# One core, one decoder layer: feed-forward operands made ahead of the change of stage, conformer norm as a task of its own

## The chip, the core and the metric

The kernel runs on one core of one Trainium2 chip. The metric is the device time of one execution in microseconds (us). Five engines work from queues of their own: PE (matmuls; its weight loads are listed as PEld), DVE (elementwise work), ACT (activations, copies with a scale), POOL, which has next to nothing to do here, and SP, whose queue issues every DMA of this kernel. Each engine takes its instructions strictly in the order in which they were emitted, so an instruction that waits also holds up all that stand behind it.

## The reference

One layer on 2048 tokens of width 1024, all in float32:

```python
h = rms_norm(x, mix_norm_g);  z = h @ w_in                    # 1024 -> 2048
lru_x, lru_gate, conf_a, conf_b = split(z, 4)                 # 512 each
y_lru = rg_lru(conv4(lru_x)) * gelu(lru_gate)
c = silu(layer_norm(conv31(conf_a * sigmoid(conf_b))))
x = x + concat(y_lru, c) @ w_out
x = x + cross_attention(rms_norm(x), mem)                     # 256 memory tokens, 4 heads
g, u = split(rms_norm(x) @ w_up, 2)                           # 1024 -> 2 x 3072
x = x + (gelu(conv3(g)) * u) @ w_down                         # 3072 -> 1024
out = rms_norm(x) * final_norm_g
```

## The kernel before

**Arithmetic.** A float32 operand is split into a rounded high part and a low part: `split` is one ACT copy (`wh`, `Xh`, `hidh`, `yh`) and one DVE subtraction (`wl`, `Xl`, `hidl`, `yl`). `mm3` then makes three matmuls, high by high, high by low, low by high. Nearly all matmuls are 128 x 128 by 128 x 512.

**Stages.** Tokens are worked in four quarters of 512. `mixer(q)` makes the input projection, the conformer convolution (31 DVE instructions for each of four channel blocks) and the LRU of a quarter. `attend(q)` first calls `conf_out`, the layer norm of the conformer branch: two sums over channels made on PE by a matrix of ones (`ps<-sum,ones`), then scale, `Silu` and split. It goes on with the output projection (`ps<-wh,yh` and the like), attention through memory tiles prepared once, the residual, and the normed and transposed rows `xn` that the feed-forward reads; these go to DRAM through `xn_kept`, and the residual through `x2_kept`. `memory_a` and `memory_vo` prepare the memory side meanwhile.

**Feed-forward.** It works on two halves `h` of 1024 tokens, each as a 2 x 2 block of Strassen's kind, seven products for eight. `halves_x(h)` reads the half's sixteen `xn` tiles, makes four combinations (`t`) for each of four contraction blocks and splits all seven operands (`B11`, `B21`, `T2`, `T1`, `T3`, `T4`, `B22`), 28 pairs of tiles. `up(h)` runs over 12 column groups `j`; each has a gate half and an up half, each of them one `strassen_cols` of seven products of 12 matmuls. Raw `w_up` columns come by DMA, are combined (`s`) and split. Its results (`cv`) go to DRAM as `hid`. `prepare_down` makes the seven combinations of `w_down` for its 3 chunks x 4 blocks, splits them (84 pairs) and stores them as `w_down2`; it is started when half 1 of the up projection begins. `down(h)` runs over 3 chunks; each has seven products, each of 4 token blocks x 12 matmuls, whose left operands are loads `h` from `hid` or combinations `s` of them, and whose right operands are loads `wh`, `wl` from `w_down2`. It adds into 16 `acc` tiles, all loaded from `x2` ahead of its first product. `finish` norms and stores.

**What sets the order.** The program is recorded by coroutines (`Task`), where `yield n` asks to be resumed after n us of recorded PE work, and a yielded task waits for that one; `drive` always steps the first due task in its list. The recorded operations then go through a planner (`Program`): buffers come from four pools of fixed slots (`SLOTS`: 82 of S, tiles of 512 columns; 4 of W, raw weights; 4 of D, tiles of 1152 columns for `cb`, `gb`, `cv`; 8 PSUM banks), granted in the order of recording, and a list scheduler places each operation on its engine by due times worked backwards from the PE order. The emitted order of each engine is what it finds. The profile gives every planned instruction the line of the one `getattr` call in `emit`, so groups are told apart by tile names.

Of the kernel before, what the change touches and what calls it, by code (L numbers as in the profile page):

```python
# [41 lines left out]
SLOTS = dict(S=82, W=4, D=4, ps=8)  # L42
# [370 lines left out]
def hybrid_layer(  # L413
# [583 lines left out]
    mixed = [None] * NQ  # L997
    attended = [Task(None) for _ in range(NQ)]
# [42 lines left out]

    def attend(q, ready):
        for t in ready:
            yield t
        C, L = mixed[q]
        Y = []
        yield from conf_out(C, Y)
# [75 lines left out]
    def halves_x(h, B):  # L1123
        for i in range(KH):
            b11, b21 = (xn_kept.get((2 * h) * NK + k) for k in (i, i + KH))
            b12, b22 = (xn_kept.get((2 * h + 1) * NK + k) for k in (i, i + KH))
            t1 = combine("t", b12[:], b11[:], ALU.subtract)
            t2 = combine("t", b22[:], t1[:], ALU.subtract)
            t3 = combine("t", b22[:], b12[:], ALU.subtract)
            t4 = combine("t", b21[:], t2[:], ALU.subtract)  # L1130
            for key, src in (("B11", b11), ("B21", b21), ("T2", t2), ("T1", t1), ("T3", t3), ("T4", t4), ("B22", b22)):
                hi, lo = pair("X")
                split(src[:], hi, lo)
                B.setdefault(key, []).append((hi, lo))
            yield 0

    def strassen_cols(c0, B, outs):
# [10 lines left out]
        def product(bank, src, key, start):  # L1148
            wh, wl = pair("w", (P, KQ, P))
            split(src, wh, wl)  # L1150
            with together():
                for k in range(KH):
                    x = B[key][k]
                    mm3(bank[:], wh[:, k, :], wl[:, k, :], x[0][:], x[1][:], start and k == 0, k == KH - 1, skip_group_check=True)

# [37 lines left out]
    def up(h, B):  # L1193
        for j in range(NCH):
# [31 lines left out]
            yield from strassen_cols(DFF + 2 * j * P, B, gated)  # L1226
# [5 lines left out]
    NCK = 3  # L1232
    KD = NF // NCK // 2
# [6 lines left out]
    def prepare_down():  # L1240
        for c in range(NCK):
            for i in range(KD):
                f = c * 2 * KD + i
                r1, r2 = (raw_rows(w_down[0], (f + j * KD) * P) for j in range(2))
                b11, b12, b21, b22 = r1[:, :TT], r1[:, TT:], r2[:, :TT], r2[:, TT:]
# [12 lines left out]
    def down(h):  # L1258

        acc = [[[x2_kept.get(((2 * h + th) * NTB + tb) * 2 + half, None, "acc") for half in range(2)] for tb in range(NTB)] for th in range(2)]  # L1260
        for c in range(NCK):
            raw = {}

            def hid(kq, th, i):
                if (kq, th, i) not in raw:
                    f = (c * 2 + kq) * KD + i
                    t = tmp("h")
                    t0 = (2 * h + th) * TT
                    pr.dma(t[:], h_kept[f * P : (f + 1) * P, t0 : t0 + TT], reads=[h_tok[h, f]])
                    raw[kq, th, i] = t  # L1270
                return raw[kq, th, i]

            s = {}

            def operand(key, i):
                if (key, i) not in s:
                    if key == "S1":
                        s[key, i] = combine("s", hid(0, 1, i)[:], hid(1, 1, i)[:], ALU.add)
                    elif key == "S2":
                        s[key, i] = combine("s", operand("S1", i)[:], hid(0, 0, i)[:], ALU.subtract)  # L1280
                    elif key == "S3":
                        s[key, i] = combine("s", hid(0, 0, i)[:], hid(0, 1, i)[:], ALU.subtract)
                    elif key == "S4":
                        s[key, i] = combine("s", hid(1, 0, i)[:], operand("S2", i)[:], ALU.subtract)
                    else:
                        return hid(*dict(A11=(0, 0), A12=(1, 0), A22=(1, 1))[key], i)
                return s[key, i]

            def product(banks, akey, bkey, start):
                L, R = [], []  # L1290
                for i in range(KD):
                    src = operand(akey, i)
                    hi, lo = pair("hid")
                    split(src[:], hi, lo)
                    L.append((hi, lo))
                    at = wd_at(c, bkey, i)
                    R.append((wd_kept.get(at, None, "wh"), wd_kept.get(at + 1, None, "wl")))
                for tb in range(NTB):
                    ts = slice(tb * P, (tb + 1) * P)
                    with together():  # L1300
                        for i in range(KD):
# [79 lines left out]
    def nothing():  # L1381
        yield 0
# [49 lines left out]
```

## Time and profile before

| | us |
|---|---|
| median of 3 runs (lowest, highest) | 2584.69 (2583.64, 2588.04) |
| the profiled execution: its time | 2585.25 |
| its span, first to last instruction | 2583.5 |
| PE busy in the span | 2481.4 (96%) |
| DVE busy | 1861.4 (72%) |
| ACT busy | 1119.9 (43%) |
| DMA moved | 522.71 MB, mean 202 GB/s |

Busy PE is the union of matmuls that overlap, and a matmul counts as busy also while the clock is halved; so the share is not the last word on how full PE is. The views of stretches give, for each engine, its busy time with the number of instructions that began in it ("x443"), the clock that TensorE was granted (1.00 is full), and how busy the DMA engines were. Comparing the number of matmuls begun in a stretch with that in a stretch that nothing disturbs gives what the stretch lost, to waits and to the clock together. The view of waits has, per pair of engine and releaser, the total in us, how often, and the longest.

### The profile page before, as it was taken

What the parts mean: (1) busy time and instruction counts of PE and PEld (TensorE: products, weight loads), DVE (VectorE), ACT (ScalarE), POOL (GpSimd) and SP (SyncE); (2) the same over time, 40 slices, a digit from 0 to 9 for tenths busy, and PEclk for the clock granted to TensorE, in tenths of its full rate; (3) what the DMA queues carried; (4) which work ended last, traced back from release to release, by engine and by line L of the source; (5) the groups of instructions that cost most, each with busy time, mean ns of one, the idle gap of its engine ahead of it and who ended that gap; (6) DMA issues with size and microseconds to landing.
All of it is one profiled execution on the core that took longest, in us unless ns stands there. A gap on an engine that the chain in (4) does not pass through costs nothing.

```text
span 2583.5 us, 32715 instructions
## 1 busy us (share of the span) xinstructions
PE 2481.4 (96%) x11300; PEld 2045.9 (79%) x11300; DVE 1861.4 (72%) x3137; ACT 1119.9 (43%) x1939; POOL 0.7 (0%) x6
## 2 busy tenths in 40 slices
PE   7999899998999999999999999899999999998998
PEld 6797788887888787878888887677788878886886
DVE  6999995099529933367667667999976765657656
ACT  6571754226333624355444445565544432223212
POOL 0000000000000000000000000000000000000000
PEclk9999999999999999999999999999999999998999
DMA  8687594855574748533222224689832197779774
GB/s 291 211 270 266 171 321 156 318 164 199 194 251 144 260 139 296 197 107 103 89 90 78 78 90 130 231 314 333 290 102 90 66 330 231 254 271 323 233 240 170
DMA packets 312764, 522.71 MB, mean 202 GB/s; under 512 B 29916, under 2 KB 107740, under 8 KB 312598
## 3 DMA queue, kind: packets, MB, share of 16 engines
q1 hardware_dynamic: 312598, 520.62, 59.1%
q8 instruction: 89, 1.46, 0.2%
q14 instruction: 77, 0.63, 0.1%
HBM read 384.19 MB, written 136.31 MB: 201 GB/s over the span
## 4 chain that ended last, share of the span: by engine, by line
PE 71%; DVE 10%; DMA 3%; issue 2%; ACT 1%; DVEq 0%; ACTq 0%; SPq 0%
PE ps L389 71%; DVE conv L389 2%; DVE wl L389 2%; DVE xc L389 1%; DVE cv L389 1%; DVE s L389 1%; DVE t L389 1%; DMA wh<-w_down 0%; DMA wl<-w_down 0%; DVE gb L389 0%; ACT xn L389 0%; DVE Xl L389 0%; DMA w_down<-wl 0%; DVE gate L389 0%; DMA w_down<-wh 0%
## 5 line engine op out<-in xcount | busy, mean ns | idle before, releaser
L389 PE MATMUL ps<-Xh,wl 128*128 128x512 f32 x1344 | 527.4, 392 | 11.1 <-DVE wl L389 11.0
L389 PE MATMUL ps<-Xh,wh 128*128 128x512 f32 x1344 | 526.6, 392 | 8.2 <-ACT wh L389 5.8
L389 PE MATMUL ps<-Xl,wh 128*128 128x512 f32 x1344 | 525.1, 391 | 0.0
L389 DVE SCALAR_TENSOR_TENSOR conv<-cb,v,conv 128x512 f32<-128x512 f32 x480 | 331.1, 739 | 0.4
L389 PEld LDWEIGHTS ps<-Xh,wl 128*128 128x128 f32 x1344 | 253.2, 188 | 72.2 <-DVE wl L389 20.2
L389 PEld LDWEIGHTS ps<-Xh,wh 128*128 128x128 f32 x1344 | 253.3, 189 | 65.1 <-ACT wh L389 11.0
L389 PEld LDWEIGHTS ps<-Xl,wh 128*128 128x128 f32 x1344 | 253.3, 188 | 52.3
L389 PE MATMUL ps<-wh,hidh 128*128 128x512 f32 x672 | 264.3, 393 | 13.8 <-ACT hidh L389 13.8
L389 PE MATMUL ps<-wh,hidl 128*128 128x512 f32 x672 | 264.1, 393 | 0.0
L389 PE MATMUL ps<-wl,hidh 128*128 128x512 f32 x672 | 263.7, 392 | 0.3 <-DMA wl<-w_down 0.2
L389 DVE TENSOR_TENSOR acc<-acc,ps 128x512 f32<-128x512 f32 x192 | 129.2, 685 | 165.8 <-PE ps L389 165.8
L389 DVE TENSOR_TENSOR wl<-raw,wh 128x512 fp32r<-128x512 f32 x276 | 183.1, 682 | 73.5 <-ACT wh L389 51.6
L389 ACT ACTIVATE wh<-raw 128x512 fp32r<-128x512 f32 x276 | 169.1, 630 | 129.2 <-PE ps L389 68.3
L389 PE MATMUL ps<-xh,wh 128*128 128x512 f32 x512 | 202.2, 395 | 3.9 <-DVE ztail L389 3.1
L389 PE MATMUL ps<-xh,wl 128*128 128x512 f32 x512 | 200.7, 392 | 0.0
L389 PE MATMUL ps<-xl,wh 128*128 128x512 f32 x512 | 200.6, 392 | 0.0
L389 ACT ACTIVATE wh<-s 128x512 fp32r<-128x512 f32 x192 | 118.8, 630 | 113.6 <-DVE s L389 68.5
L389 DVE TENSOR_TENSOR wl<-s,wh 128x512 fp32r<-128x512 f32 x192 | 129.8, 686 | 47.0 <-ACT wh L389 45.5
L389 PEld LDWEIGHTS ps<-wh,hidh 128*128 128x128 f32 x672 | 127.5, 190 | 42.0 <-ACT hidh L389 15.7
L389 ACT ACTIVATE junk<-x 128x512 f32<-128x512 f32 x96 | 60.6, 631 | 215.0 <-DVE x L389 204.0
L389 ACT ACTIVATE u<-ps 128x512 f32<-128x512 f32 x144 | 85.9, 596 | 155.7 <-PE ps L389 150.3
L389 PEld LDWEIGHTS ps<-wh,hidl 128*128 128x128 f32 x672 | 127.2, 189 | 28.8 <-DVE hidl L389 2.6
(190 smaller groups left out, 4310.9 us busy)
## 6 DMA issues: line engine op xcount, KB each, us to landing
raw<-in_w_up_dram SPq DMA_DIRECT2D x96, 512.0 KB
wh<-w_down SPq DMA_DIRECT2D x168, 256.0 KB
wl<-w_down SPq DMA_DIRECT2D x168, 256.0 KB
wh<-w_in SPq DMA_DIRECT2D x96, 256.0 KB
wl<-w_in SPq DMA_DIRECT2D x96, 256.0 KB
hid<-cv SPq DMA_DIRECT2D x48, 512.0 KB
h<-hid SPq DMA_DIRECT2D x96, 256.0 KB
w_down<-wh SPq DMA_DIRECT2D x84, 256.0 KB
```

What stands on the lines that cost most here:

```text
L389: getattr(e, name)(*[resolve(a) for a in args], **{k: resolve(a) for k, a in kw.items()})
```

## The change

- `SLOTS`: S from 82 to 85, D from 4 to 3.
- `conf_out` moves from the start of `attend(q)` into a new task `normed(q)`. For quarter 0 it waits for `mixers[0]` and 40 us; for quarter 1 for `mixers[2]` and `attended[0]`; for quarter 2 for `mixers[3]` and `attended[1]`; for quarter 3 for `normed(2)` and 55 us. `attend(0)` no longer waits for `mixers[1]`.
- `halves_x` becomes the class `HalfX`, which makes an operand when asked. For half 0 the first four operands (`first_x`) are made while the last attention runs, the others when first used. For half 1 the task `kept` makes the four combinations during half 0 of the up projection and stores them to DRAM (`tx`); in the last `strassen_cols` of half 0, `used(key)` splits the half 1 operand of a key as soon as half 0 has used that key.
- `prepare_down` starts with half 0 in place of half 1, is paced with `yield 8` in place of `yield 2`, and loads its raw rows into S tiles (`wd`, four of 256 KB) in place of W tiles (two of 512 KB).
- `down` becomes the class `Down`. `ahead` makes the operands of its first two products during the last `strassen_cols` of half 1. An `acc` tile is loaded when first added to. Half 1 takes the chunks in reverse and begins each with the seventh product, so its first product takes over the weights `wh`, `wl` that half 0 used last.

The diff, cut to its core:

```diff
-SLOTS = dict(S=82, W=4, D=4, ps=8)
+SLOTS = dict(S=85, W=4, D=3, ps=8)
...
+    def normed(q, ready, wait):
+        for t in ready:
+            yield t
+        yield wait
         C, L = mixed[q]
         Y = []
         yield from conf_out(C, Y)
+        mixed[q] = Y, L
...
+        def kept(self):
+            keys = ("T2", "T1", "T3", "T4")
+            k = Kept("tx", 4 * KH, F32)
+            yield attends[NQ - 1]
+            for i in range(KH):
+                b = {key: self.one(key, i) for key in ("B11", "B12", "B22")}
+                t1 = combine("t", b["B12"][:], b["B11"][:], ALU.subtract)
...
+                k.put(i, t2[:])
+                k.put(KH + i, t1[:])
+                yield 20
...
         def product(bank, src, key, start):
+            X = B.get(key)
             wh, wl = pair("w", (P, KQ, P))
...
+            if used:
+                used(key)
...
+    PACE = 8
...
     def prepare_down():
+        yield attends[NQ - 1]
...
-                    yield 2
+                    yield PACE
...
-        acc = [[[x2_kept.get(((2 * h + th) * NTB + tb) * 2 + half, None, "acc") for half in range(2)] for tb in range(NTB)] for th in range(2)]
...
+        def ahead(self, c, n, given=None):
+            self.given = {(c, n): given} if given else {}
+            self.ready[c, n] = self.gather(c, n)
...
+        def add(self, banks, th, half):
+            for tb in range(NTB):
+                at = (th, tb, half)
+                if at not in self.acc:
+                    self.acc[at] = x2_kept.get(((2 * self.h + th) * NTB + tb) * 2 + half, None, "acc")
...
     def feed_forward():
-        yield attended[3]
-        B = {}
-        yield from halves_x(0, B)
-        yield from up(0, B)
-        yield attends[3]
-        B = {}
-        yield from halves_x(1, B)
+        yield first
+        yield attended[NQ - 1]
+        spawn(X[1].kept(), tail)
         spawn(prepare_down(), tail)
-        yield from up(1, B)
-        del B
+        yield from up(0, X[0], X[1].make)
+        downs = [Down(h) for h in range(NH)]
+
+        def ahead(key):
+            if key in ("B21", "T1"):
+                downs[0].ahead(0, ("B21", "T1").index(key))
+
+        yield from up(1, X[1], ahead)
         for h in range(NH):
-            acc = yield from down(h)
-            tasks.insert(0, Task(finish(h, acc)))
+            yield from downs[h].run(downs[h + 1] if h < NH - 1 else None)
+            tasks.insert(0, Task(finish(h, downs[h].acc)))
```

How the emitted order moves, at three places. First SP's queue where the up projection of half 1 ends and the down projection begins; `hid<-cv` are stores of the up projection, all else loads. Before:

```order
L389 DMA raw<-in_w_up_dram 128x4x256 x2
L389 DMA hid<-cv 128x1024 x2
L389 DMA acc<-x_88 128x512 x16
L389 DMA h<-hid 128x512 x2
L389 DMA wh<-w_down_91 128x512
L389 DMA wl<-w_down_91 128x512
L389 DMA wh<-w_down_91 128x512
```

And now:

```order
L389 DMA raw<-in_w_up_dram 128x4x256 x2
L389 DMA h<-hid 128x512
L389 DMA hid<-cv 128x1024
L389 DMA wh<-w_down_91 128x512
L389 DMA wl<-w_down_91 128x512
L389 DMA h<-hid 128x512
L389 DMA hid<-cv 128x1024
L389 DMA wh<-w_down_91 128x512
```

The sixteen `acc` loads stood ahead of the first `h`; now 24 loads (8 `h`, 8 `wh`, 8 `wl`) stand ahead of the first `acc`, and the first of them ahead of two stores of the up projection.

Second DVE's queue where half 1 of the up projection takes over; `t` are half 1's combinations, `Xl` its split operands, `gb`, `up` and `cv` are still work of half 0's last column group. Before:

```order
L389 TENSOR_TENSOR up<-u,ps 128x512
L389 TENSOR_TENSOR t<-xn,t 128x512
L389 TENSOR_TENSOR t<-xn 128x512
L389 TENSOR_TENSOR cv<-cv,up 128x512
L389 TENSOR_TENSOR t<-xn,t 128x512
L389 TENSOR_TENSOR Xl<-xn,Xh 128x512 x3
L389 TENSOR_TENSOR Xl<-t,Xh 128x512
L389 TENSOR_TENSOR t<-xn 128x512 x2
```

And now:

```order
L389 TENSOR_TENSOR gb<-u,ps 128x512
L389 TENSOR_TENSOR Xl<-xn,Xh 128x512 x2
L389 TENSOR_TENSOR wl<-t,wh 128x512
L389 TENSOR_TENSOR Xl<-xn,Xh 128x512
L389 TENSOR_TENSOR wl<-raw,wh 128x512
L389 TENSOR_TENSOR Xl<-xn,Xh 128x512
L389 TENSOR_TENSOR gb<-u,ps 128x512
```

The combinations are gone from this place (the `t` of `wl<-t` belongs to `prepare_down`), and the first `Xl` stand among the last adds of the gate half (`gb`), where they stood behind the first `up` of the up half.

Third PE's queue where attention of quarter 2 ends; `xn` is transposed there for the feed-forward, `sum,ones` is the conformer norm of quarter 3 and `wh,yh` its output projection. Before:

```order
L389 MATMUL ps<-wl,pth 128x512
L389 MATMUL ps<-wh,ptl 128x512
L389 MATMUL ps<-ident,xn 128x128 x16
L389 MATMUL ps<-sum,ones 128x512
L389 MATMUL ps<-ident,xn 128x128 x16
L389 MATMUL ps<-wh,yh 128x512
```

And now, around the first transposes, with 33 matmuls of the same output projection ahead of these rows, up to the last of `ptl`:

```order
L389 MATMUL ps<-wh,yh 128x512
L389 MATMUL ps<-wl,yh 128x512
L389 MATMUL ps<-wh,yl 128x512
L389 MATMUL ps<-ident,xn 128x128 x16
L389 MATMUL ps<-wh,yh 128x512
```

The two `sum,ones` of quarter 3 have moved far ahead, into the attention of quarter 2, and 36 matmuls of the output projection now stand between the last matmul with `ptl` and the first transposes.

More of the change, by code (lines that the diff above doesn't have):

```diff
@@ L997, in hybrid_layer @@
     mixed = [None] * NQ
+    started = [Task(None) for _ in range(NQ)]
     attended = [Task(None) for _ in range(NQ)]
@@ L1040, in mixer @@
         mixed[q] = C, L
+    def normed(q, ready, wait):
+        for t in ready:
+            yield t
+        yield wait
+        C, L = mixed[q]
+        Y = []
+        yield from conf_out(C, Y)
+        mixed[q] = Y, L
     def attend(q, ready):
@@ L1044, in attend @@
             yield t
-        C, L = mixed[q]
-        Y = []
-        yield from conf_out(C, Y)
+        Y, L = mixed[q]
+        started[q].done = True
         xs = load_x(q, "x1")
@@ L1121, in combine @@
         return t
[L1123 to L1131, printed above, removed]
+    UP_ORDER = ("B11", "B21", "T2", "T1", "T3", "T4", "B22")
@@ L1243, in prepare_down @@
                 f = c * 2 * KD + i
-                r1, r2 = (raw_rows(w_down[0], (f + j * KD) * P) for j in range(2))
-                b11, b12, b21, b22 = r1[:, :TT], r1[:, TT:], r2[:, :TT], r2[:, TT:]
+                raw = []
+                for r0 in (f * P, (f + KD) * P):
+                    for half in range(2):
+                        t = tmp("wd")
+                        pr.dma(t[:], w_down[0, r0 : r0 + P, half * TT : (half + 1) * TT])
+                        raw.append(t[:])
+                b11, b12, b21, b22 = raw
                 t1 = combine("t", b12, b11, ALU.subtract)
@@ L1255, in prepare_down @@
                     wd_kept.put(at + 1, lo[:])
-                    yield 2
-    def down(h):
-        acc = [[[x2_kept.get(((2 * h + th) * NTB + tb) * 2 + half, None, "acc") for half in range(2)] for tb in range(NTB)] for th in range(2)]
[L1261 to L1301, printed above, removed]
-                            mm3(banks[tb][:], L[i][0][:, ts], L[i][1][:, ts], R[i][0][:], R[i][1][:], start and i == 0, i == KD - 1, skip_group_check=True)
-                    yield 0
-            def add(banks, th, half):
-                for tb in range(NTB):
-                    t = acc[th][tb][half]
-                    V("tensor_tensor", t[:], t[:], banks[tb][:], op=ALU.add)
-            pa = [ps() for _ in range(NTB)]
-            yield from product(pa, "A11", "B11", True)
-            add(pa, 0, 0)
-            pb = [ps() for _ in range(NTB)]
-            yield from product(pb, "A12", "B21", True)
-            add(pb, 0, 0)
-            yield from product(pa, "S2", "T2", False)
-            add(pa, 0, 1)
-            pb = [ps() for _ in range(NTB)]
-            yield from product(pb, "S1", "T1", True)
-            add(pb, 1, 1)
-            yield from product(pa, "S3", "T3", False)
-            add(pa, 1, 0)
-            add(pa, 1, 1)
-            yield from product(pb, "S4", "B22", False)
-            add(pb, 0, 1)
-            pa = [ps() for _ in range(NTB)]
-            yield from product(pa, "A22", "T4", True)
-            add(pa, 1, 0)
-        return acc
@@ L1340, in finish @@
                 for half in range(2):
-                    st.add(tb, half, acc[th][tb][half][:])
+                    st.add(tb, half, acc[th, tb, half][:])
             r = st.rstd()
@@ L1345, in finish @@
                 for half in range(2):
-                    t = acc[th][tb][half]
+                    t = acc[th, tb, half]
                     V("scalar_tensor_tensor", t[:], t[:], r[:, tb : tb + 1], g[half][:], op0=ALU.mult, op1=ALU.mult)
```

157 lines of the change are left out of this document (144 added, 13 removed).

## The prediction

> **What bounds the kernel now.** I read the page first. PE is busy in nearly the whole span, and the chain that ended last is mostly matmuls:
>
> ```profile
> span 2583.5 us, 32715 instructions
> PE 2481.4 (96%) x11300; PEld 2045.9 (79%) x11300; DVE 1861.4 (72%) x3137; ACT 1119.9 (43%) x1939; POOL 0.7 (0%) x6
> PE 71%; DVE 10%; DMA 3%; issue 2%; ACT 1%; DVEq 0%; ACTq 0%; SPq 0%
> ```
>
> The change takes no matmul away, so it can only win time in which PE stands or runs at half clock. Next I read the stretches around each change of stage, with two quiet ones to compare (columns: PE, PEld, DVE, ACT, POOL busy with instructions begun, granted clock, DMA share, GB/s):
>
> ```profile
> 245.00:345.00 100.00, 89.22 (x377) 71.63 (x376) 98.05 (x166) 68.80 (x113) 0.00 (x0) 0.93 0.63 211
> 560.00:620.00 60.00, 52.04 (x215) 41.58 (x214) 60.00 (x101) 50.66 (x79) 0.00 (x0) 0.91 0.69 227
> 985.00:1005.00 20.00, 15.48 (x70) 11.94 (x69) 6.35 (x12) 13.91 (x27) 0.00 (x0) 0.83 1.02 380
> 1140.00:1160.00 20.00, 15.76 (x68) 11.63 (x67) 14.51 (x25) 16.88 (x33) 0.00 (x0) 0.91 0.28 101
> 1200.00:1300.00 100.00, 100.00 (x443) 82.85 (x442) 69.21 (x109) 44.90 (x64) 0.00 (x0) 1.00 0.24 79
> 1600.00:1640.00 40.00, 31.89 (x121) 23.28 (x120) 39.33 (x67) 23.64 (x41) 0.00 (x0) 0.91 0.46 150
> 1640.00:1860.00 220.00, 213.08 (x918) 170.13 (x917) 214.59 (x342) 130.56 (x209) 0.00 (x0) 1.00 0.88 309
> 1860.00:2060.00 200.00, 200.00 (x883) 165.53 (x883) 148.96 (x230) 90.49 (x134) 0.00 (x0) 1.00 0.31 105
> 2060.00:2140.00 80.00, 74.84 (x317) 60.35 (x316) 53.19 (x80) 27.34 (x41) 0.00 (x0) 0.96 0.84 299
> 2340.00:2380.00 40.00, 31.02 (x117) 23.17 (x116) 32.22 (x53) 12.40 (x20) 0.00 (x0) 0.83 1.02 366
> ```
>
> A quiet stretch begins 443 matmuls in 100 us, one each 0.2257 us. Where all are of that size, the matmuls missing tell the loss, waits and clock together. 1600 to 1640: 177.2 - 121 = 56.2, 12.7 us. 1640 to 1860: 974.6 - 918 = 56.6, 12.8 us. 2060 to 2140: 354.4 - 317 = 37.4, 8.4 us. 2340 to 2380: 177.2 - 117 = 60.2, 13.6 us. In the other stretches sizes are mixed, so I add the idle time and the clock's share: 985 to 1005: 4.5 + 0.17 x 20 = 7.9 us; 1140 to 1160: 4.2 + 1.8 = 6.0; 560 to 620: 8.0 + 5.4 = 13.4; 245 to 345: 10.8 + 7.0 = 17.8. That is 92.6 us at eight places. Who ended the waits, over the whole span:
>
> ```profile
> PE ps L389 <- DVE wl L389: 15.1, 17, 3.1
> PE ps L389 <- ACT hidh L389: 13.8, 4, 4.8
> PE ps L389 <- DVE sum L389: 11.2, 2, 8.0
> PE ps L389 <- ACT wh L389: 7.1, 6, 3.5
> PE ps L389 <- ACT xn L389: 5.5, 6, 4.1
> ```
>
> They are the splits of weights, the splits of the down projection's left operands, the conformer sums and `xn`: those that the change moves.
>
> **The middle of the up projection (12.7 and 12.8 us).** DVE is the late engine: 39.33 of 40 us, then 214.59 of 220, against 69.21 of 100 in the quiet half. Each of its instructions on 512 columns costs this:
>
> ```profile
> L389 DVE TENSOR_TENSOR wl<-raw,wh 128x512 fp32r<-128x512 f32 x276 | 183.1, 682 | 73.5 <-ACT wh L389 51.6
> L389 ACT ACTIVATE wh<-raw 128x512 fp32r<-128x512 f32 x276 | 169.1, 630 | 129.2 <-PE ps L389 68.3
> ```
>
> At the change of half DVE has 16 combinations and 28 `Xl` to do beside its stream: 44 x 0.682 = 30.0 us. The combinations go (10.9 us, into half 0), and the 28 splits (19.1 us) begin one `strassen_cols` earlier and are spread over 84 matmuls, 19.0 us of PE. At 69% of its stream DVE has 5.9 us to spare there; so it falls some 13 us behind in place of the 30 - 5.9 = 24 us now, which cost 12.7 us, so that about 11.5 us of lead must have been absorbed. I keep 1.7 of the 12.7 us: a gain of 11.0.
>
> `prepare_down` has 84 `wl` and 48 combinations, 132 x 0.682 = 90 us of DVE, and 84 x 0.630 = 52.9 us of ACT. Now it stands in the 220 us from 1640. Paced at 8 us, 84 steps take 672 us of PE work, from about 1142: 13.4 us of DVE per 100, ending near 1814. Half 0's quiet 69.21 becomes 82.6, for the first 160 us 89.4 with `kept`'s combinations; ACT goes from 44.90 to 52.8. Both are below the 97.5% at which the present stretch loses 5.8 us per 100. I take 11.3 of the 12.8 us as won and charge 3.0 us for new small waits in half 0 (bounds: nothing, as in the quiet stretch, and 5.8 per 100 over 460 us, 26.7). SP's queue gets 44 more transfers for `tx` and re-read `xn`, 16 of them stores, and 24 more for the halved raw loads; DMA runs at 24% there, so they hide.
>
> **The down projection (8.4 and 13.6 us).** In SP's and ACT's queue at the first change (the number ahead of the engine is a length):
>
> ```profile
> 2077.63 4.95 SPq L389 DMA_DIRECT2D acc<-x  x8
> 2082.86 0.99 SPq L389 DMA_DIRECT2D h<-hid  x2
> 2084.21 0.32 SPq L389 DMA_DIRECT2D wh<-w_down  x1
> 2084.88 0.32 SPq L389 DMA_DIRECT2D wl<-w_down  x1
> 2117.81 2.38 ACT L389 ACTIVATE hidh<-s 128x512 fp32r<-128x512 f32 x4 [2.01 <-DVE s L389]
> ```
>
> The last eight `acc` take 2077.63 to 2082.86, 0.65 us each; loads then go out every 0.67 us, the queue's pace when full. Sixteen `acc` are 10.5 us ahead of the first `h`. The first three products need 16 `h` and 24 weights, 40 x 0.67 = 26.8 us, and last 3 x 48 x 0.2257 = 32.5 us; with `acc` it is 37.3, 4.8 us too long, and a wait of 4.8 us ends with `hidh<-s`. Now the operands of two products (24 loads) are asked for before the up projection ends, and `acc` comes four at a time. Their cover is the quiet end of the up projection (DMA share 0.31 from 1860 to 2060); were it gone, the 4.8 us and its half-clock time would return. Gain 7.2 of 8.4. At half 1 the same pile-up stands at 2340 (DMA share 1.02). Its first product now takes over eight weight tiles (8 x 0.67 = 5.4 us of queue), its `h` are made one product earlier, and its 16 `acc` (10.5 us) are spread. Together 15.9 us, more than the 13.6 lost; I keep 1.1: gain 12.5.
>
> **The start of the feed-forward (6.0 us).** Sixteen of 28 `X` pairs are made ahead, 16 x (0.682 + 0.630) = 21 us of DVE and ACT, while attention leaves both idle (DVE 6.35 of 20 us from 985). The 28 pairs and the raw weights now meet in 1140 to 1160, where ACT is busy 16.88 of 20. Twelve pairs remain there: gain 4.0.
>
> **Conformer norm.** At 985 PE waits 4.1 us for `xn` and then runs at half clock; 36 matmuls, 36 x 0.2257 = 8.1 us, now stand in between, and need only old operands: gain 7.0 of 7.9. For quarter 1, DVE is busy 60.00 of 60 us, so moving its sums only lets DVE reach the last `yl` sooner by the work set behind it; summed in the two orders with durations as above this is 3 us for the first pair, 1 for the second: gain 2.0. For quarter 0 the sign turns. DVE is full there too (98.05), and PE's cover shrinks: 48 matmuls of the memory side (24 of 512 columns, 24 of 256, together 8.3 us) move behind the softmax, while DVE reaches the first `yl` only 3.6 us sooner by the same sum. It now has this to spare:
>
> ```profile
> 333.17 1.28 DVE L389 TENSOR_TENSOR yl<-conv,yh 128x512 fp32r<-128x512 f32 x2
> 336.27 0.39 PE L389 MATMUL ps<-wh,yh 128*128 128x512 f32 x1
> ```
>
> 336.27 - 334.45 = 1.8 us. So 8.3 - 3.6 - 1.8 = 2.9 us are lost, call it 3.0 (bounds: a gain of 1, if the memory side's splits had been the brake, and a loss of 8.3).
>
> ACT gets 16 more table loads, 86 for 70, as `Silu` now comes among other functions:
>
> ```profile
> L389 ACT ACT_TABLE_LOAD x70 | 89.8, 1283 | 77.2 <-DVE small L389 46.3 <-issue 14.9 <-PE ps L389 12.9
> 328.26 1.28 ACT L389 ACT_TABLE_LOAD   x1
> 329.56 0.72 ACT L389 ACTIVATE conv<-conv,v 128x512 f32<-128x512 f32 x1
> ```
>
> 1.30 us from one start to the next, 16 x 1.30 = 20.8 us on an engine that is busy 43%; I charge 2.0 us (bounds 0 and 20.8). The Trainium skill, "ScalarE: Activation LUTs", section "What ACT_TABLE_LOAD costs", adds a drain and gives about 2.66 us for every change of set. By that the 16 would be 42.6 us of ACT, an estimate from that page, and my charge would double; the row above shows no drain, and I go by the row. D with three slots lets one `cb` or `gb` wait for its pair's other user; I cost it at nothing, as DVE and not PE is ahead there, and take it up as a rival.
>
> **Sum.** Gains 11.0 + 11.3 + 7.2 + 12.5 + 4.0 + 7.0 + 2.0 = 55.0; charges 3.0 + 3.0 + 2.0 = 8.0; net 47.0. From the profiled execution's 2585.25 us (its span of 2583.5 and 1.75 around it, 0.6 above the median of the three) this is 2538 us.
>
> **Rivals.** *More is won:* the kept remainders (1.7, 1.5, 1.2, 1.1, 2.0, 0.9) and the charges vanish, 16.4 us: 2522. For it speaks how quiet DVE is in attention; against it, that planned orders so far left a rest at every change of stage.
>
> *The pile-up stays in the down projection:* the queue is full at 1.02, and spread loads may only wait elsewhere. The 19.7 us return: 2558. It decides if each product's 12 or 16 loads, 8 to 10.7 us, no longer fit its 10.8 us.
>
> *The conformer pays more:* with D at three, the second `cb` of a pair waits for a convolution of another, 31 instructions of this kind,
>
> ```profile
> L389 DVE SCALAR_TENSOR_TENSOR conv<-cb,v,conv 128x512 f32<-128x512 f32 x480 | 331.1, 739 | 0.4
> ```
>
> 22.9 us, and holds its PSUM bank. PE has one projection, 84 to 96 matmuls, 19 to 21.7 us, to go on with; up to 4 us is left over, three times, 12 us: 2550. DVE at 98.05 speaks for it, the slack from 345 on against.
>
> *Slower:* the first half is starved of S slots. X[0] holds 56 of 85 (28 pairs); `wd`, `t` and the pairs waiting for their stores take more, and weight splits get too few to run ahead. PE then waits at each product as it does from 1640. My sum leaves 4.5 us for this in both halves. The 47.0 us are gone when it takes 51.5 us of the 920 us of up projection, 5.6 per 100, just under the 5.8 from 1640 to 1860; from there on the change is slower, and at 7.0 per 100 it is 64.4 us, 59.9 more than I have: 2598. Against it: the present loss comes at 97.5% of DVE, not from slots.
>
> *Nothing moves:* the waits were where operands land, and they land as late as now: 2585.
>
> **How the numbers follow.** Chances: forecast 0.51, more is won 0.13, the pile-up 0.13, the conformer 0.14, slower 0.05, nothing 0.04. The first four end faster by over 0.2% (5.2 us, about what a measurement of this kernel can tell from no change): 0.91; the fifth gives slower 0.05, the last same 0.04. The range takes in 2522 and 2558 with 3 us of the unknown charges at either end: 2519 to 2561. It leaves out slower, nothing, and a little of the rest, some 0.15.
>
> **What would show it.** Right: around the middle of the up projection about 443 matmuls per 100 us and a clock of 1.00; `PE <- ACT hidh` down from 13.8 us to under 3; `PE <- ACT xn` under 2; `w_down` stores from about 1140 on; DVE near 83% in half 0. Wrong: in half 0 `PE <- DVE wl` in every group of columns; a DMA share over 1 and a halved clock at the start of either down half; `DVE sum` or `DVE yl` with more than 15 us together.

## The result, and the profile after

The changed kernel takes 2538.92 us (median of 4 runs, 2538.64 to 2539.22); the kernel before, on the same chip, 2585.15 us (4 runs, 2583.64 to 2588.04). The ratio is 0.982 (95% interval 0.9803 to 0.9837): faster by 46 us, where 47 were forecast. The profiled execution took 2539.05 us. That the sum came out is not to say that its terms did, and they are taken one by one further down.

The page of the changed kernel: span, busy engines, and the chain that ended last.

```profile
span 2537.3 us, 32865 instructions
PE 2463.0 (97%) x11300; PEld 2040.5 (80%) x11300; DVE 1872.4 (74%) x3137; ACT 1136.8 (45%) x1955; POOL 0.7 (0%) x6
PE 79%; DVE 13%; DMA 4%; ACT 3%; issue 2%; SPq 0%; DVEq 0%; ACTq 0%
```

The number of matmuls is the same, and the chain is now 79% PE where it was 71%. About half of DVE's 13% of the chain is the convolution (`conv` has 6% of the span there). In the table below, the named places that still lose are those ahead of the up projection, and its middle. The stretches of the changed kernel that answer to those of before (columns as there; the two of the down projection lie 30 and 40 us earlier than before, 560 to 640 is longer, and 60 to 100 and 1140 to 1180 are new):

```profile
60.00:100.00 40.00, 35.51 (x171) 29.17 (x170) 39.87 (x76) 14.99 (x27) 0.00 (x0) 0.91 0.55 191
245.00:345.00 100.00, 88.14 (x357) 69.08 (x356) 96.37 (x162) 61.62 (x85) 0.00 (x0) 0.91 0.55 183
560.00:640.00 80.00, 75.78 (x323) 59.87 (x323) 80.00 (x139) 66.49 (x101) 0.00 (x0) 1.00 0.58 190
985.00:1005.00 20.00, 20.00 (x96) 16.71 (x96) 3.09 (x6) 10.21 (x20) 0.00 (x0) 1.00 0.77 279
1140.00:1160.00 20.00, 16.79 (x89) 13.61 (x88) 12.96 (x23) 18.57 (x34) 0.00 (x0) 1.00 0.79 259
1140.00:1180.00 40.00, 34.83 (x165) 27.86 (x164) 32.95 (x54) 33.57 (x58) 0.00 (x0) 1.00 0.66 220
1200.00:1300.00 100.00, 100.00 (x443) 82.80 (x442) 89.12 (x142) 51.40 (x78) 0.00 (x0) 1.00 0.64 216
1600.00:1640.00 40.00, 36.63 (x158) 28.93 (x157) 40.00 (x66) 26.50 (x46) 0.00 (x0) 1.00 0.73 249
1640.00:1860.00 220.00, 220.00 (x973) 182.15 (x972) 180.70 (x279) 108.98 (x168) 0.00 (x0) 1.00 0.49 163
2030.00:2110.00 80.00, 80.00 (x355) 66.24 (x354) 56.70 (x87) 27.44 (x43) 0.00 (x0) 1.00 0.89 308
2300.00:2340.00 40.00, 40.00 (x178) 33.14 (x177) 31.89 (x53) 11.70 (x22) 0.00 (x0) 1.00 1.01 362
```

At 443 matmuls per 100 us, the stretch from 1600 now lacks 177.2 - 158 = 19 matmuls (4.3 us, where it was 12.7), and 1640 to 1860 and both changes to a half of the down projection lack none. Half 0 of the up projection lacks none either, with DVE at 89.12 of 100. The last row shows that a DMA share of 1.01 costs nothing by itself: 178 matmuls of 178 begin, at a clock of 1.00.

The largest waits of PE in the changed kernel, over the whole span (rows for first loads and for shorter waits are left out):

```profile
PE ps L389 <- DVE wl L389: 10.3, 9, 4.6
PE ps L389 <- DVE sum L389: 4.6, 2, 2.5
PE ps L389 <- DVE cb L389: 4.5, 2, 4.3
PE ps L389 <- ACT xn L389: 1.4, 5, 0.3
```

`ACT hidh`, 13.8 us before, is gone from the list; `xn` fell from 5.5 to 1.4. A new name is among them: `cb`, nearly all of it a single wait of 4.3 us.

**Where the time went, place by place.** PE does nearly the same work in nearly the same order in both kernels. So each of the 11,300 matmuls can be given its undisturbed pace in these traces (0.227 us for 512 columns, 0.120 for 256, 0.109 for 128), and what the trace took beyond this is booked at the place in the work where it arose. The last column names the experiment, told below, that puts one part back, with what that place loses in it.

| place (start to end in us of undisturbed PE work) | before | after | won | forecast | with one part put back |
|---|---|---|---|---|---|
| quarter 0, up to its attention (60 to 450) | 36.5 | 44.2 | -7.7 | -5.0 | u_norm 43.2, u_slots 36.8, u_s82 45.2 |
| quarter 1, norm (530 to 560) | 11.6 | 5.9 | 5.7 | 2.0 | u_norm 5.9, u_slots 11.3, u_s82 10.7 |
| quarter 3, norm and `xn` (905 to 930) | 8.7 | 0.0 | 8.7 | 7.0 | u_norm 9.7 |
| start of the feed-forward (1045 to 1075) | 7.2 | 6.7 | 0.5 | 4.0 | u_first 9.2, v_xn 6.2 |
| half 0 of the up projection (1200 to 1500) | -0.4 | -0.4 | 0 | -3.0 | |
| middle of the up projection (1500 to 1540) | 13.3 | 4.6 | 8.7 | 11.0 | u_x1 10.0, u_prep 4.1 |
| half 1 of the up projection (1540 to 1955) | 11.3 | -0.6 | 11.9 | 11.3 | u_prep 8.6 |
| first change of the down projection (1955 to 2060) | 8.3 | -0.2 | 8.5 | 7.2 | u_acc 2.6, u_down 2.1, u_ahead -0.1 |
| half 1 of the down projection (2210 to 2250) | 13.8 | -0.1 | 13.9 | 12.5 | u_down 10.2, u_slots 6.9, u_order 0.9 |
| all other places | 42.2 | 45.9 | -3.7 | 0 | |
| sum (by the spans 2583.5 - 2537.3 = 46.2) | 152.5 | 106.0 | 46.5 | 47.0 | |

The forecast of -5.0 for quarter 0 is its charge of 3.0 and the 2.0 for table loads. Places that none of the edits touches differ by up to 2 us between kernels (800 to 905: 3.9 in the changed kernel, 5.5 in u_first, v_xn, u_down and u_prepdown), so a difference at a place counts from some 2 us on. The waits and the clock in the rows above give the same picture with coarser numbers.

### The profile page after: what moved, and what is told of

It is laid out like the page before. It is cut to its first block, busy times and chain, and to the rows that moved or that the text cites. A ratio compares the mean times of both kernels' runs of the same rounds, so it can differ in the third digit from the quotient of the medians.

```text
span 2537.3 us, 32865 instructions
## 1 busy us (share of the span) xinstructions
PE 2463.0 (97%) x11300; PEld 2040.5 (80%) x11300; DVE 1872.4 (74%) x3137; ACT 1136.8 (45%) x1955; POOL 0.7 (0%) x6
## 4 chain that ended last, share of the span: by engine, by line
PE 79%; DVE 13%; DMA 4%; ACT 3%; issue 2%; SPq 0%; DVEq 0%; ACTq 0%
PE ps L389 79%; DVE conv L389 6%; DVE xc L389 1%; ACT L389 1%; DMA wh<-w_in 1%; DVE wl L389 1%; DVE gate L389 1%; DMA x<-in_x_dram 1%; DVE Xl L389 1%; DVE x L389 0%; DVE yl L389 0%; ACT gate L389 0%; DMA raw<-in_w_out_dram 0%; ACT wh L389 0%; DMA wl<-VO 0%
## 5 line engine op out<-in xcount | busy, mean ns | idle before, releaser
L389 DVE TENSOR_TENSOR acc<-acc,ps 128x512 f32<-128x512 f32 x192 | 129.5, 685 | 152.5 <-PE ps L389 152.3
L389 ACT ACTIVATE wh<-raw 128x512 fp32r<-128x512 f32 x240 | 146.3, 633 | 104.0 <-PE ps L389 43.9
L389 DVE TENSOR_TENSOR wl<-raw,wh 128x512 fp32r<-128x512 f32 x240 | 160.7, 685 | 33.0 <-ACT wh L389 17.6
L389 DVE TENSOR_TENSOR x<-x,ps 128x512 f32<-128x512 f32 x64 | 43.6, 683 | 141.8 <-PE ps L389 141.7
```

What stands on the lines that cost most here:

```text
L389: getattr(e, name)(*[resolve(a) for a in args], **{k: resolve(a) for k, a in kw.items()})
```

## The experiments

All are the changed kernel with one edit, except where said. Each time is a median; the ratio is to the kernel before on the same chip, whose median was 2586.47 us for the first four, 2585.2 for the second four and 2586.17 for the last four. Intervals are about 0.0015 (4 us) to either side, so a difference below that is told from the place that it shows up at, not from the time. A is the account of the prediction; the other letters are the rivals in the texts quoted.

### u_prep: prepare_down in half 1 again

```diff
-    PACE = 8
+    PACE = 2
...
-        spawn(prepare_down(), tail)
         yield from up(0, X[0], X[1].make)
+        spawn(prepare_down(), tail)
```

> The changed kernel with prepare_down started with half 1 again and paced at 2 us. Theory A (each change of stage lost time for a cause of its own): the small waits for wl come back where prepare_down now meets the weight splits, 12.8 us over some 220 us, and 3 to 6 us more at the middle of the up projection; both changes to the down projection stay without a wait: 2554 to 2558 us. Rival B (one cause: the DVE work of prepare_down in half 1 makes everything behind it late, and the other edits add nothing): the 34.8 us from the middle of the up projection on come back, the waits for hidh too: 2570 to 2576 us.

2546.55 us, ratio 0.9844 (0.9829 to 0.9859). The stretch behind the middle:

```profile
1640.00:1860.00 220.00, 215.81 (x932) 173.05 (x931) 216.23 (x343) 129.57 (x211) 0.00 (x0) 1.00 0.88 309
```

DVE is back at 216.23 of 220 us, and 974.6 - 932 = 43 matmuls (9.6 us) are missing; the middle itself does not care (4.1 us by the table, 4.6 in the changed kernel). So the small waits of half 1 are `prepare_down`'s, as A has it, but they are 9.2 us by the table and not the 11.3 of before; both expected ranges, 2554 to 2558 for A and 2570 to 2576 for B, were too high. B falls.

### u_x1: half 1's X made at the change

```diff
-        spawn(X[1].kept(), tail)
...
-        yield from up(0, X[0], X[1].make)
+        yield from up(0, X[0])
+        for key in UP_ORDER:
+            X[1].make(key)
+            yield 0
```

> The changed kernel with the seven operands of half 1 made where half 1 begins (no kept, no used in half 0). Theory A: 44 DVE instructions meet there again, 30.0 us, but without prepare_down beside them; 6 to 10 us come back between 1600 and 1640, nothing elsewhere: 2545 to 2549 us. Rival B: with prepare_down out of the way DVE has the room: under 2 us, 2539 to 2541 us.

2542.48 us, ratio 0.9829 (0.9814 to 0.9844), a little under A's 2545 to 2549. The middle of the up projection:

```profile
1600.00:1640.00 40.00, 34.34 (x134) 26.52 (x133) 39.68 (x68) 23.77 (x42) 0.00 (x0) 0.91 0.33 111
```

134 matmuls for the changed kernel's 158: 5.4 us come back by the table, at the place that A names and nowhere else. The clock is 0.91 again.

### u_acc: sixteen acc loaded ahead of each half

```diff
         def run(self, last=None):
+            for th in range(2):
+                for tb in range(NTB):
+                    for half in range(2):
+                        self.acc[th, tb, half] = x2_kept.get(((2 * self.h + th) * NTB + tb) * 2 + half, None, "acc")
```

> The changed kernel with the 16 acc tiles of each half loaded ahead of its first product again. Theory A (the queue is the cause in the down projection): 10.5 us of loads ahead of the others; 1 to 4 us come back at the first change, where two products' operands are there already, and 3 to 8 at the second: 2543 to 2551 us, as waits for hidh with a DMA share over 1. Rival B: no more than 1 us, 2539 to 2540 us.

2541.96 us, ratio 0.9827 (0.9813 to 0.9842), just below A's 2543 to 2551. The first change of the down projection:

```profile
2040.00:2120.00 80.00, 78.06 (x343) 63.67 (x342) 55.45 (x85) 26.75 (x42) 0.00 (x0) 1.00 0.88 306
```

354.4 - 343 = 11 matmuls are missing, 2.6 us; half 1 of the down projection loses 1.0. Against the changed kernel's -0.2 and -0.1, sixteen loads ahead of the first `h` cost 3.9 us in all where the other measures stay.

### u_ahead: no down operands made ahead

```diff
-        yield from up(1, X[1], ahead)
+        yield from up(1, X[1])
```

> The changed kernel without the down operands made during the last strassen_cols of half 1; acc stays spread. Theory A: h and weights of the first two products, 24 loads of 0.67 us, start about 19 us later; 1 to 5 us come back at the first change alone: 2540 to 2544 us. Rival C (in the down projection the spreading of acc is all, and asking ahead is idle): under 0.5 us, 2539 us.

2537.09 us, ratio 0.9811 (0.9794 to 0.9827): no slower. The first change of the down projection, where 354 matmuls of 354 begin:

```profile
2040.00:2120.00 80.00, 80.00 (x354) 66.24 (x353) 54.21 (x83) 25.25 (x39) 0.00 (x0) 1.00 0.90 323
```

C, the theory that this step is idle beside the others, is right; A expected a loss.

### u_order: the old order of chunks and products, no weights taken over

```diff
-            self.order, self.given = list(range(NCK))[:: -1 if h else 1], {}
+            self.order, self.given = list(range(NCK)), {}
...
-                if self.h:
+                if False:
...
-                if not self.h:
+                if True:
...
-            yield from downs[h].run(downs[h + 1] if h < NH - 1 else None)
+            yield from downs[h].run()
```

> The changed kernel with both halves of the down projection in the old order of chunks and products, so that half 1 takes over no weights and has nothing made ahead; acc stays spread, half 0's first operands stay ahead. Theory A (amended after the first runs: spread acc is worth only 1.1 us at the change of half): the taken-over weights and the order remove the 13.8 us there, so 8 to 14 us come back at half 1 of the down projection: 2547 to 2553 us. Rival C (spread acc is enough by itself, either measure makes the other idle): under 2 us, 2539 to 2541 us.

2539.67 us, ratio 0.9824 (0.981 to 0.9839). Half 1 of the down projection:

```profile
2320.00:2360.00 40.00, 39.58 (x174) 32.16 (x173) 25.73 (x42) 10.24 (x17) 0.00 (x0) 1.00 1.05 382
```

174 of 177 matmuls, 0.9 us by the table. The weights taken over and the order with them spare 1.0 us and no more: C again.

### u_down: the three down measures undone together

The edits of u_acc, u_ahead and u_order at once.

> The changed kernel with all of the old down projection: 16 acc ahead of each half, nothing made ahead, the old order. Theory A: the 8.4 and 13.6 us come back whole, for they arise in the down projection itself: 2559 to 2562 us. Rival D (they came in part from what the up projection of half 1 left behind, with prepare_down's stores in the queue): under 14 us come back, below 2553 us.

2551.09 us, ratio 0.9867 (0.9852 to 0.9882): below 2553, as D has it, and not A's 2559 to 2562. Its two changes of a half:

```profile
2040.00:2120.00 80.00, 78.65 (x345) 64.26 (x344) 53.51 (x81) 27.08 (x41) 0.00 (x0) 1.00 0.94 335
2320.00:2360.00 40.00, 34.73 (x133) 26.64 (x132) 26.24 (x43) 12.47 (x20) 0.00 (x0) 0.87 0.98 353
```

Half 1 loses 10.2 us again: idle 5.3 us and the clock behind that (0.87, 5.2 us). Alone, the three undone measures cost 3.9 us (u_acc), nothing (u_ahead) and 1.0 us (u_order); together 12.6 (2.3 at the first change and 10.3 at the second): each covers for the others. At the first change only 2.3 of the 8.5 us won come back. So most of the prediction's 7.2 us for that place does not depend on the steps that it gave, as long as the rest of the change stands; u_prepdown below tries the cause that D names.

### u_norm: the conformer norm inside attention again

```diff
     def normed(q, ready, wait):
...
-        C, L = mixed[q]
-        Y = []
-        yield from conf_out(C, Y)
-        mixed[q] = Y, L
...
-        Y, L = mixed[q]
+        C, L = mixed[q]
+        Y = []
+        yield from conf_out(C, Y)
...
-    attends[0] = spawn(attend(0, [normeds[0]]))
+    attends[0] = spawn(attend(0, [mixers[1]]))
```

(and the other three quarters likewise)

> The changed kernel with conf_out at the start of attend again and attend's old conditions; all else changed. Theory A: quarter 1 and quarter 3 lose 5.7 and 8.7 us again, the window of quarter 0 gains 7.7 (the loss there comes from PE reaching the output projection of quarter 0 earlier than DVE its operands): 2545 to 2547 us. Rival E (the loss in quarters 0 and 1 comes from the third D slot alone): it stays, 2551 to 2555 us.

2544.87 us, ratio 0.9847 (0.983 to 0.9863): at the lower edge of A's 2545 to 2547, but not by A's places, and far from E's 2551 to 2555, though the loss of quarter 0 stays as E has it. Quarter 0, quarter 1 and quarter 3 of it:

```profile
245.00:345.00 100.00, 87.22 (x367) 69.29 (x367) 98.65 (x171) 65.22 (x106) 0.00 (x0) 0.91 0.59 199
560.00:640.00 80.00, 76.93 (x324) 60.22 (x322) 80.00 (x140) 66.48 (x101) 0.00 (x0) 0.98 0.57 190
985.00:1005.00 20.00, 14.96 (x63) 11.30 (x62) 6.65 (x12) 13.71 (x26) 0.00 (x0) 0.83 1.00 342
```

Quarter 3 has its loss back (9.7 us by the table, idle 5.0 us and a clock of 0.83). But quarter 1 stays as good as in the changed kernel (324 matmuls, 323 there), and quarter 0 stays as bad (idle 12.8 us and a clock of 0.91). Moving the norm did neither; it is worth quarter 3 alone. This called for the next two runs.

### u_slots: the old slots, S 82 and D 4

```diff
-SLOTS = dict(S=85, W=4, D=3, ps=8)
+SLOTS = dict(S=82, W=4, D=4, ps=8)
```

> The changed kernel with the old slots, S 82 and D 4. Theory A: the loss of 7.7 us up to the attention of quarter 0 is that of the norm's new place, so the old slots return little of it, under 3 us; three S slots less cost up to 2 elsewhere: 2537 to 2540 us. Rival E (a cb that waits for a slot holds a PSUM bank, and PE waits for it): the wait for cb near 82 us goes and 4 to 8 us come back: 2531 to 2535 us.

2548.24 us, ratio 0.9861 (0.9846 to 0.9875): 10.6 us slower than the changed kernel, by the two ratios. Both theories, A with 2537 to 2540 and E with 2531 to 2535, missed; what E says of quarter 0 came true. Three stretches, and the wait of PE from 560 to 640:

```profile
60.00:100.00 40.00, 37.84 (x189) 30.58 (x188) 39.80 (x75) 18.98 (x35) 0.00 (x0) 1.00 0.71 240
560.00:640.00 80.00, 72.03 (x305) 58.13 (x304) 80.00 (x131) 57.29 (x93) 0.00 (x0) 0.94 0.53 179
2320.00:2360.00 40.00, 36.29 (x147) 29.07 (x146) 27.18 (x44) 12.34 (x20) 0.00 (x0) 0.91 0.97 347
```
```profile
PE ps L389 <- DVE sum L389: 8.0, 1, 8.0
```

The loss of quarter 0 is gone (36.8 by the table, 36.5 before), that of quarter 1 is back (idle 8.0 us, clock 0.94), and half 1 of the down projection lacks 177.2 - 147 = 30 matmuls, 6.8 us, with every measure of the change in place. Two pools were changed at once, so one more run had to part them.

### u_s82: S 82, D 3

```diff
-SLOTS = dict(S=85, W=4, D=3, ps=8)
+SLOTS = dict(S=82, W=4, D=3, ps=8)
```

> The changed kernel with S 82 and D 3, to part the two slot edits. Theory A (D rules the conformer stages, S the down projection): the loss up to the attention of quarter 0 stays near 44 us and that of quarter 1 near 6, while 5 to 7 us come back at half 1 of the down projection: 2544 to 2547 us. Rival E2 (S rules them too): quarter 1 loses 11 us again and quarter 0 gains 7, 2541 us or below with the down projection clean.

2559.69 us, ratio 0.99 (0.9885 to 0.9915). Both theories, A with 2544 to 2547 and E2 with at most 2541, missed the time by far, each right at some places: A at quarter 0 and in the down projection, E2 at quarter 1. The same three stretches, and the longest wait of PE from 560 to 640:

```profile
60.00:100.00 40.00, 35.78 (x172) 29.09 (x171) 39.15 (x75) 14.74 (x27) 0.00 (x0) 0.91 0.59 204
560.00:640.00 80.00, 72.56 (x303) 56.81 (x302) 80.00 (x140) 67.18 (x101) 0.00 (x0) 0.96 0.54 184
2320.00:2360.00 40.00, 36.17 (x147) 29.08 (x147) 31.85 (x52) 10.41 (x18) 0.00 (x0) 0.91 1.04 370
```
```profile
PE ps L389 <- DMA wh<-w_out: 4.7, 1, 4.7
```

With D at three quarter 0 loses whatever S is (171 and 172 matmuls from 60, for 188 and 189 with four); with S at 82 quarter 1 and the down projection lose whatever D is (303 and 305 matmuls; 147 and 147). So the two are told apart: at 82 S slots the fourth D slot is worth 0.0039 of the time, 10 us (u_s82 against u_slots), and at three D slots three S slots are worth 0.008, 21 us (u_s82 against the changed kernel), at many places: 7.0 us in the down projection, 4.8 at the norm of quarter 1, 2 to 4 each from 800, 1045 and 1500 on. Quarter 1 loses alike with either D, but not by the same wait: with four D slots it is the old 8.0 us for `sum`, with three that is 0.3 us, and a late load `wh<-w_out` takes 4.7.

### u_first: no operand of half 0 made early

```diff
-    EARLY = 4
+    EARLY = 0
```

> The changed kernel with none of half 0's operands made ahead (EARLY 0). Theory F (the prediction's term): the start of the feed-forward loses 4 us more, 10 to 12 in place of 6.7: 2542 to 2544 us. Rival G (ACT's own work on quarter 3's xn and xt, 16 x 0.65 us in one queue with the weight splits, sets that start): under 1.5 us more, 2538 to 2540 us.

2538.77 us, ratio 0.982 (0.9806 to 0.9835): as the changed kernel, and in G's 2538 to 2540. The start of the feed-forward, and the row of its longest wait:

```profile
1140.00:1180.00 40.00, 33.54 (x154) 26.75 (x153) 35.21 (x58) 33.22 (x59) 0.00 (x0) 0.96 0.60 204
```
```profile
1153.35 0.50 PE L389 MATMUL ps<-Xh,wh 128*128 128x512 f32 x1 [4.39 <-ACT wh L389]
```

At the place itself 2.5 us come back (154 matmuls for 165), less than F's 4 and more than G's 1.5; they do not show in the time, for the place before it (930 to 1045) loses 2.6 less than in the changed kernel.

### v_xn: xn of the last quarter scaled by DVE

```diff
-                ACT(t[:], xs[tb][half][:], AF.Copy, scale=r2[:, tb : tb + 1])
+                if q == NQ - 1:
+                    V("tensor_scalar", t[:], xs[tb][half][:], r2[:, tb : tb + 1], None, op0=ALU.mult)
+                else:
+                    ACT(t[:], xs[tb][half][:], AF.Copy, scale=r2[:, tb : tb + 1])
```

> The changed kernel with the eight scalings that make xn of quarter 3 done by DVE in place of ACT. Rival G: ACT's queue is 5 us shorter where the feed-forward starts, DVE is idle then, so 2 to 4 of the 6.7 us go: 2535 to 2537 us. Theory F: nothing, 2538 to 2540 us.

2537.99 us, ratio 0.9816 (0.98 to 0.9832), not told apart from the changed kernel. The start of the feed-forward:

```profile
1140.00:1160.00 20.00, 16.90 (x89) 13.53 (x87) 16.36 (x32) 16.61 (x32) 0.00 (x0) 1.00 0.76 260
```

ACT fell from 18.57 to 16.61 us and DVE rose from 12.96 to 16.36, and the place loses 6.2 for 6.7: what ACT no longer delays, DVE does. G's 2535 to 2537 counted on a gain there that did not come.

### u_prepdown: old down projection and old prepare_down together

The edits of u_down and u_prep at once.

> The changed kernel with the old down projection and with prepare_down in half 1 again. Theory D (what was lost at the start of the down projection came from prepare_down's tail in the up projection of half 1 together with the late loads): 6 to 8 us come back there in place of the 2.1 seen with the old down projection alone, 10 to 14 at its half 1, and 9.2 from prepare_down itself: 2564 to 2570 us. Rival H (it came from something else that changed, such as slots or raw rows): the first stays near 2: 2557 to 2562 us.

2559.93 us, ratio 0.9901 (0.9886 to 0.9915): inside H's 2557 to 2562, below D's 2564 to 2570. The first change of the down projection:

```profile
2040.00:2120.00 80.00, 78.65 (x338) 64.08 (x337) 53.32 (x82) 26.54 (x41) 0.00 (x0) 0.98 0.86 307
```

The first change loses 3.9 us now by the table (u_down 2.3), the second 10.1 as in u_down. So the first change does not get its whole old loss back: 4.6 of the 8.3 us are not accounted for. Three S slots fewer are the obvious candidate, but in u_s82 that place loses nothing while the down measures stand; the old down projection was not run with 82 slots, so this stays open.

## Why the prediction was right, and where it was not

Time and range held, and so did the mechanism in the up projection and for quarter 3; that of the down projection held in part, and that of quarters 0 and 1 did not. The two sides of the sum were each off, by about the same amount, and that they cancel to within 1 us is luck. The three S slots, for which the sum has no term, carry 21 us of the time.

**Half 1 of the up projection (11.3, measured 11.9)** is shown as told: `prepare_down` is 9.2 of it, and its cover in half 0 holds. DVE there is 89.12 of 100 against a worked-out 82.6 to 89.4, ACT 51.40 against 52.8. The charge of 3.0 for new small waits in half 0 was nothing: 443 matmuls begin in 100 us.

**The middle (11.0, measured 8.7)**: right in kind, too large. "In place of the 24 us now" DVE was to fall 13 us behind, within an absorbed lead of 11.5; DVE is busy 40.00 of 40 us, and a rest of 4.6 stays where 1.7 was kept. The step is at odds with the one behind it: it gives DVE 5.9 us to spare from the 69% of the kernel before, while `prepare_down` is to stand beside it. At the 89.12% measured in half 0, 19 us leave 2.1 to spare, and the same sum gives a rest of 19.1 - 2.1 - 11.5 = 5.5 us. That fits, but is not shown: in u_prep `prepare_down` stands behind the middle, and the place still loses 4.1. u_x1 returns 5.4 us, so the splits and combinations are the larger part; the rest was not told apart.

**The down projection (7.2 + 12.5, measured 8.5 + 13.9)**: the places and sizes are right, the steps not. Taking the 24 loads asked for ahead as a term of the gain is wrong: without them nothing is lost (u_ahead). Spreading `acc` alone is worth 3.9, the new order with the weights taken over 1.0; undone together 12.6. And half 1 needs the three S slots just as much: 7.0 us return without them. No step of the prediction named S slots as a gain; it named their lack as its way to a slower kernel. That rival's place was the up projection; there, at 85 slots, nothing is starved.

**The norm of quarter 3 (7.0, measured 8.7)** is shown by u_norm, which loses 9.7 at that place. Some of the gain is lost again beside it: the neighbouring places from 800 and 930 lose 4 us more than before, 2 of which are within what untouched places vary.

**The norm of quarter 1 (2.0, measured 5.7)** failed as an explanation: with the norm back in attention the gain stays, with 82 S slots it goes. The runs show no single cause behind it: the wait for `sum` is 8.0 us in both kernels with four D slots and at most 2.1 in those with three, and with 82 S slots a wait for a load stands in its place (u_s82).

**Quarter 0 (-3.0 and -2.0, measured -7.7)** failed in the same way. "D with three slots … I cost it at nothing" is the step that was wrong, and the rival *the conformer pays more* had the mechanism. The kernel before from 60 to 100, and in DVE's timeline the two `cb` of a pair, three us apart:

```profile
60.00:100.00 40.00, 37.82 (x188) 30.59 (x187) 39.80 (x76) 18.71 (x35) 0.00 (x0) 1.00 0.69 236
```
```profile
66.29 0.69 DVE L389 TENSOR_TENSOR cb<-ps,sg 128x512 f32<-128x512 f32 x1 [0.20 <-PE ps L389]
...
69.42 0.68 DVE L389 TENSOR_TENSOR cb<-ps,sg 128x512 f32<-128x512 f32 x1
```

In the changed kernel, the same two of DVE with the copy that fills the head of the second one's tile, and the matmuls of PE that wanted a PSUM bank (the figure in brackets is the wait):

```profile
66.47 0.68 DVE L389 TENSOR_TENSOR cb<-ps,sg 128x512 f32<-128x512 f32 x1
...
85.34 0.17 DVE L389 COPY cb<-ctail 128x30 f32<-128x30 f32 x1
...
85.68 0.68 DVE L389 TENSOR_TENSOR cb<-ps,sg 128x512 f32<-128x512 f32 x1
```
```profile
86.42 1.12 PE L389 MATMUL ps<-ident,mem 128*128 128x128 f32 x4 [4.25 <-DVE cb L389]
```

The second `cb` stands 16 us later, behind a convolution of the pair before. In the kernel before, and in u_slots, all four of these copies run within the first 2.6 us; here three do, and the fourth comes only at 85.34, when a slot is free. All that time the product stays in its PSUM bank, and PE waits 4.25 us for it. The clock adds its part: from 60 to 100, PE is idle for 4.5 us and the clock is 0.91, 0.09 x 40 = 3.6 us, 8.1 together; with four D (u_slots) it is 2.2 and nothing. That is 5.9 us; from 245 to 345 another 3.1 (11.9 + 9.0 for 10.8 + 7.0 before). The rival's sum had 4 us of wait three times; it was one wait of 4.25 and the clock behind it. From 245 to 345 PE waits only 0.3 us for `cb`, and 6.3 for `wl` (4.1 before); that the loss there is the missing slot's too is likely, as u_slots loses 16.5 us there (20.9 in the changed kernel), but in which way is not shown.

That clock bears on every price here. In u_first one wait of 4.39 us leaves 0.96 over 40 us, 1.6 us on top; at the same place in the changed kernel no wait is longer than 1.74 us, and the clock is 1.00. The longest wait alone does not decide it: in u_acc, u_ahead and u_order it is 1.7 us there too, and the clock is 0.96. The Trainium skill, "TensorE: Matmul & The Clock Gate", section "What's actually happening", has the clock halve after an idle window of about 3.4 us and return after a busy one. The traces agree in size: 1.6 us is about the price of one such window at half clock (1.7, an estimate from the Trainium skill), and the 3.6 us from 60 to 100 that of two. They do not bear out a wait of 3.4 us as the condition, as those three runs show, and what else counts was not tried.

The norm's own move costs quarter 0 nothing (u_norm 43.2, and 41.9 to 44.2 in the others with the same slots). The 3.0 us charged to it had the right sign for a wrong reason.

**The table loads** were counted right, 86 of them:

```profile
L389 ACT ACT_TABLE_LOAD x86 | 110.3, 1283 | 59.7 <-issue 35.4 <-DVE small L389 22.2 <-PEq L1530 0.7
```
```profile
329.28 1.28 ACT L389 ACT_TABLE_LOAD   x1
330.57 1.34 ACT L389 ACTIVATE conv<-conv,v 128x512 f32<-128x512 f32 x2
```

1.29 us from one start to the next, again without a drain. No loss at any place could be put down to them; the 2.0 us charged are within what places vary.

**The start of the feed-forward (4.0, measured 0.5)** is the term that failed. The step was that 16 pairs made ahead relieve ACT in 1140 to 1160. ACT is busier there than before, 18.57 us for 16.88:

```profile
1144.05 4.39 ACT L389 ACTIVATE xn<-x,small 128x512 f32<-128x512 f32 x7
...
1150.41 2.99 ACT L389 ACTIVATE xt<-ps,v 128x512 f32<-128x512 f32 x5
1153.26 0.66 ACT L389 ACTIVATE wh<-s 128x512 fp32r<-128x512 f32 x1
...
1154.35 0.67 ACT L389 ACTIVATE wh<-wd 128x512 fp32r<-128x512 f32 x1
1154.87 2.23 ACT L389 ACTIVATE Xh<-t 128x512 fp32r<-128x512 f32 x4
```

```profile
1153.97 0.50 PE L389 MATMUL ps<-Xh,wh 128*128 128x512 f32 x1 [1.74 <-ACT wh L389]
```

The row of `wh<-s` is the one that PE waits 1.74 us for; ahead of it stand the `xn` and `xt` of the last rows, and behind it `prepare_down`'s first `wh<-wd` and the first four of the twelve `Xh` that the early ones left over. The first 20 us do look better (89 matmuls for 68, at full clock), and the prediction's own window would have booked 2.8 us as won. But over 40 us before and after are level: 163 matmuls before,

```profile
1140.00:1180.00 40.00, 35.76 (x163) 28.47 (x162) 31.63 (x50) 32.86 (x56) 0.00 (x0) 0.96 0.42 143
```

and 165 now: the waits moved 10 us on. A window that ends inside a stage shows where a loss went from, not that it went. u_first still loses 2.5 us more at the place, so the early operands do win something there; what takes it back was not told apart.

So 57.9 us were won at the places that the sum named, against its 55.0, and 11.4 were lost elsewhere, against its 8.0: 7.7 in quarter 0, 3.7 at all other places together.

**What stays open**: the 4.6 us at the first change of the down projection; which of ACT, DVE and SP's queue would have to give for the start of the feed-forward; what the changed kernel would do with four D and 85 S slots: the fourth D slot was worth 10 us at 82 S slots, at 85 it was not tried, and room for it would have to come from another pool; and which tiles lack the three S slots, for u_slots and u_s82 show where time is lost without them, and not how. Each edit also lets the planner lay out the rest anew, so a few us at a place may be its doing. No run was faster than the changed kernel by more than the interval.

## What to carry to other kernels

A count of buffer slots is a term of the sum like any other: three slots more of one pool were worth 21 us here (with three D slots), and one less of another cost 10 (with 82 S slots), about as much as the largest single rearrangement, and both hid behind edits that looked like the cause. When several measures protect the same change of stage, undo each alone and all together: here three measures are worth 3.9, 0 and 1.0 us alone and 12.6 together. Cost what is left at a stage as well as what is taken away, over a window that reaches past the stage; an engine that gets room there may be filled by the next work in its queue.

## What the runs showed that was not expected

A DMA share over 1 at the change of a half costs PE nothing where the operands are asked for early enough (1.01 and 178 of 178 matmuls); the prediction had taken it, with a halved clock, as a sign of failure. SP's queue can be held up while the DMA engines have room (a share of 0.32 from 1122 to 1140). In the changed kernel's timeline just ahead of the feed-forward, on SP (the figure after the start is how long SP took over the rows) and on DVE:

```profile
1122.47 17.82 SPq L389 DMA_DIRECT2D x<-x  x4
1140.38 0.38 SPq L389 DMA_DIRECT2D xn<-xn  x1
```
```profile
1139.25 0.69 DVE L389 TENSOR_TENSOR x<-x,ps 128x512 f32<-128x512 f32 x1 [0.68 <-PE ps L389]
```

Four stores of the residual `x` take 17.82 us to issue, against 0.38 us for one transfer that is ready. The last of them comes out when the add of 1139.25 is done, and all that stands behind the stores waits as well. Whether a wait of PE hangs on that was not tried.
